# Local attention scores of a tile in one step over four PSUM banks instead of two steps over two banks each

## The chip, the cores and the metric

The kernel runs on one core of a Trainium2 chip, as one launch. The metric is the device time of the launch in microseconds (us), lower is better. Engines are named as in the profile: PE is TensorE (PEld its weight loads), DVE is VectorE, ACT is ScalarE, POOL is GpSimd, SP is SyncE, which issues nearly all DMAs.

## The reference

One layer of a streaming encoder on 2048 prompt tokens and 8 x 16 tokens of running streams (17 tiles of 128 tokens), model width 1024, all in float32. What the change touches is the local attention of the prompt: 8 query heads share 2 key/value heads of width 64, a chunk of 64 tokens sees itself and the two chunks before it, and each head has a learned sink in the softmax's denominator.

```python
def band_attend(q, k, v, mask, sinks):
    s = jnp.einsum('bnlkgd,bnskd->bnkgls', q, k) * (A_HEAD_DIM ** -0.5)
    s = jnp.where(mask, s, -jnp.inf)
    mx = jnp.maximum(jnp.max(s, axis=-1, keepdims=True), sink)
    p = jnp.exp(s - mx)
    p = p / (jnp.sum(p, axis=-1, keepdims=True) + jnp.exp(sink - mx))
    return jnp.einsum('bnkgls,bnskd->bnlkgd', p, v)
...
qm, km, vm, om, ip, fp, qa, ka, va = split_in(x @ w_in)
hm = og * head_norm(mlstm_chunkwise(...))          # matrix memory, 4 heads x 128
ha = swa_prompt(rope(qa), rope(ka), va, attn_sinks)
mix = jnp.concatenate([hm, ha], axis=-1) @ w_out
h = layer_norm(DEEPNORM_ALPHA * x + mix, ln1_g, ln1_b)
f = conv_ffn(h, ...)                               # up, causal convolution, silu gate, down
y = layer_norm(DEEPNORM_ALPHA * h + f, ln2_g, ln2_b)
```

## The kernel before

**Stages.** Four follow each other on TensorE. The input projection (`i_dense`, lines L770 and L798) goes over four blocks of tokens. The output projection (`o_block`, L232 to L234) goes over five blocks, [16, 0, 1], [2..5], [6..9], [10..13] and [14, 15], counted here from 0 to 4. Then come the feed-forward's up projections (`f_ups`, L1949) and down projections (`f_downs`, L2153). Products in float32 are made of three products of a high and a low part (`split`: ScalarE casts to the high part at L227, VectorE subtracts for the low part at L228). The matmuls of these stages are called dense here; their banks are named dps, fup and fht.

**Chains.** The sequence part runs between the dense matmuls of the first two stages, as three generators: `t_sample` (the running streams), `m_chain` (the matrix memory of the prompt, tile by tile) and `a_chain` (the local attention of the prompt, tile by tile). `Chains.weave` keeps a clock of its own: each dense piece adds its cost in nanoseconds, and a chain makes its next step when its due time has come. A step yields (its cost on TensorE, the delay until its next step, the number of banks that the next step needs).

**Banks.** Chains share five PSUM banks (`NBANKS`, pool `tps`). Each request (`bank`) enters in a list when the planner holds that bank to be free again: now plus `HOLDS[name]`, or 3500 ns for a name that isn't there. A step that needs n banks waits until the n oldest entries have passed. TensorE's order is written down as the program is made; the order on the other engines is set by a scheduler from the program's order and its own estimates of time. [...]

**One tile of attention** (`swa`). `swa_first` turns queries and keys by transposes (pq, pk) and splits them. `scores(j0)` makes two of the four query heads of each key head: 12 matmuls into two banks (psc, L1389, operands of 64 rows), then mask and row maximum on VectorE (L1393, one operation per head, into sc), then the sink. `exps` takes the exponentials on ScalarE (L1404), `divided` the quotients (L1410). The probabilities are turned by TensorE (ppt, L1432), copied by ScalarE (pth, L1433) and multiplied with the values (ppo, L1438); a copy (mixa, L1445) and a DMA to zmix end the tile. The steps stand like this:

```python
z = [scores(0)]
yield 900, 3200, 2
exps(*z[0])
z.append(scores(2))
yield 900, 3600
exps(*z[1])
divided(*z[0])
...
yield 0, 3000
divided(*z[1])
```

Of the matrix memory's tile the text names pscore and pkt (L1215, L1226), pnum and pcu (L1300 on), pgr (rows of gates, L1073), pht (turned result, L1267; ScalarE copies it to mixm at L1270) and pcol (L1092; VectorE copies it to col at L1095).

**From the chains to the next stage.** Output block b + 1 reads zmix in four pieces (`x_pair`, DMA xraw), which are cast (oh, L965) and reduced to low parts (ol, L966, VectorE or POOL; VectorE alone for block 4) in the last round of block b. `x_pair` first lets the chains run on until the tiles that it reads are written. Its results are added to the input (ymix, L1724), normed in steps (`norm`: L1657, L1647 to L1650, L1661, L1663) and stored to zh. Once no chain is left, block 3's loop frees the chains' memory and banks and starts `prepare`: ScalarE issues six loads of normed tiles (hst, L1801), 18 steps later TensorE transposes them (fht, L1810) and ScalarE copies them (hraw, L1811), one transpose group per step, and then the first feed-forward block's tokens are summed and split (`f_tokens`: hraw at L1825 to L1829, hh and hl of 1536 columns), one such piece every four steps. The loop over block 4 goes on with `prepare`, and after it an assertion says that `prepare` is finished.

Of the kernel before, what the change touches and what calls it, by code (L numbers as in the profile page):

```python
# [14 lines left out]
P = 128  # L15
# [16 lines left out]
RING = 3  # L32

NBANKS = 5
HOLDS = {"pm": 6500, "pgr": 4000, "pnum": 5000, "ppo": 6500}

WB = 4

# [166 lines left out]
class Prog:  # L205
# [30 lines left out]
    def run(self):  # L236
        PS = bass.MemoryType.PSUM
        nb = len(OBLOCKS)
        with ExitStack() as es:
            def enter(*a, **k):  # L240
                cm = self.pool(*a, **k)
                return cm.__enter__(), cm
            close = lambda cm: cm.__exit__(None, None, None)
            self.cp = es.enter_context(self.pool("const"))
            self.dp = es.enter_context(self.pool("dram", space=bass.MemoryType.DRAM))
            es.enter_context(self.tc.manual_schedule(engines={mybir.EngineType.PE}))
            self.setup()
            self.wp = es.enter_context(self.pool("wsb"))
            self.dps = es.enter_context(self.pool("dps", 3, PS))
            self.tp, tcm = enter("tsb", side="right")  # L250
            self.tps, tpcm = enter("tps", 5, PS)
            self.xp, xcm = enter("xsb")
            self.skew(self.xp, 256)
            self.mp, mcm = enter("isb")
            chains = Chains(self)
            self.xs, self.gates, self.i_done = {}, {}, 0
            self.i_begin()
            self.warm_up()
            chains.weave(self.i_dense())
            close(mcm)  # L260
            wx, wxcm = enter("wx1sb")
            self.skew(wx, 448)
            self.unit_more(wx)
            self.mp, mcm = enter("osb")
            self.o_setup()
            for b in range(nb - 2):
                chains.weave(self.late_done(self.o_block(b)))

            def prepare():
                first = self.f_hT(0)  # L270
                next(first)
                for _ in range(18):
                    yield
                for _ in first:
                    yield
                for s in (1, "t1", "t3", 7, "t2", 6):
                    self.f_tokens(0, s)
                    for _ in range(4):
                        yield

            made, n = None, 0
            for cost in self.late_done(self.o_block(nb - 2)):
                chains.weave([cost])
                if made is None:
                    if not chains.live:
                        close(tpcm)
                        close(tcm)
                        self.fp, fcm = enter("fsb", side="right")
                        self.fup, fpcm = enter("fup", 3, PS)
                        self.f_setup()  # L290
                        made = prepare()
                else:
                    next(made, None)
            assert made is not None
            for i, _ in enumerate(self.o_block(nb - 1)):
                next(made, None)

                if i >= 22 and n < (2, 4, 5)[min((i - 22) // 4, 2)]:
                    self.f_next()
                    n += 1  # L300
            assert next(made, self) is self and not self.norms
            close(mcm)
            close(wxcm)
            close(xcm)

            self.wx, wxcm = enter("wx2sb")
            self.skew(self.wx, 704)
            self.f2, f2cm = enter("f2sb")
            self.f3, f3cm = enter("f3sb")
            self.f_ups(n)  # L310
            self.skew(self.f2, 448)
            close(f3cm)
            close(f2cm)
            self.f2, f2cm = enter("dsb")
            self.f_downs()
            for cm in (f2cm, wxcm, fpcm, fcm):
                close(cm)
# [678 lines left out]
    def bank(self, shape, name):  # L996
        self.chains.ask(HOLDS.get(name, 3500))
        return self.tps.tile(shape, F32, name=name, tag="tb")
# [360 lines left out]
    def swa(self, t):  # L1359
        nc = self.nc  # L1360
        V = nc.vector
        if self.a_first is None:
            self.swa_first(t)
            yield 550, 4000, 2
        qh, ql = self.a_first
        self.a_first = None
        r = t % RING
        if t == 0:
            slots, nk = [0], 1
            mask = self.mswa[:, :P]  # L1370
            sel = slice(0, 1)
        else:
            slots, nk = sorted([(t - 1) % RING, r]), 2
# [5 lines left out]
        def scores(j0):  # L1379

            sink = [x.rearrange("p (k j) -> p k j", k=2)[:, :, j0:j0 + 2] for x in (self.sink, self.nsink)]
            sc = self.work("sc", [P, 4, 2 * P], bufs=2)
            mx, es, sm = [self.work(n, [P, 4], bufs=2) for n in ("amx", "aes", "asm")]
            ps = [self.bank([P, 2, 2, P], "psc") for _ in range(2)]
            for j in range(2):
                for i, (q, k) in enumerate(((qh, self.kh), (qh, self.kl), (ql, self.kh))):
                    for kvh in range(2):
                        rs = slice(64 * kvh, 64 * kvh + 64)
                        nc.tensor.matmul(ps[kvh][:, j, :nk], q[rs, j0 + j], k[rs, sel], start=i == 0, stop=i == 2)  # L1389
            for kvh in range(2):  # L1390
                for j in range(2):
                    c = 2 * kvh + j
                    V.tensor_tensor_reduce(out=sc[:, c, :N], in0=ps[kvh][:, j, :nk].rearrange("p a b -> p (a b)"), in1=mask, scale=1.0, scalar=-3e38,  # L1393
                                           op0=ALU.add, op1=ALU.max, accum_out=mx[:, c:c + 1])

            w = lambda x: x.rearrange("p (k j) -> p k j", k=2)
            V.scalar_tensor_tensor(w(mx), w(mx), -0.125, sink[1], op0=ALU.mult, op1=ALU.min)
            V.tensor_add(w(es), sink[0], w(mx))
            return sc, mx, es, sm

        def exps(sc, mx, es, sm):
            nc.scalar.activation(es, es, AF.Exp)
            for j in range(4):
                nc.scalar.activation(sc[:, j, :N], sc[:, j, :N], AF.Exp, bias=mx[:, j:j + 1], scale=0.125, accum_out=sm[:, j:j + 1])  # L1404

        def divided(sc, mx, es, sm):
            V.tensor_add(sm, sm, es)
            V.reciprocal(sm, sm)
            for j in range(4):
                nc.scalar.activation(sc[:, j, :N], sc[:, j, :N], AF.Copy, scale=sm[:, j:j + 1])  # L1410

        z = [scores(0)]
        yield 900, 3200, 2
        exps(*z[0])
        z.append(scores(2))
        yield 900, 3600
        exps(*z[1])
        divided(*z[0])
        if t + 1 < NPT and self.i_done > self.place(t + 1)[0]:
# [7 lines left out]
        for kt in range(nk + 1):  # L1427
            new = self.work("pth", [P, 2, 512], bufs=2) if kt < nk else None
            for kvh in range(2) if kt < nk else ():
                pp = self.bank([P, 512], "ppt")  # L1430
                for j in range(4):
                    nc.tensor.transpose(pp[:, j * P:(j + 1) * P], scs[j // 2][:, 2 * kvh + j % 2, kt * P:(kt + 1) * P], self.ident)  # L1432
                nc.scalar.copy(new[:, kvh], pp)  # L1433
            if kt:
                po = po or self.bank([P, 512], "ppo")
                for kvh in range(2):
                    w = self.kv[slots[kt - 1]][:, P + 64 * kvh:P + 64 * kvh + 64]
                    nc.tensor.matmul(po[64 * kvh:64 * kvh + 64], w, pts[:, kvh], start=kt == 1, stop=kt == nk)  # L1438
            pts = new
            if kt == 0 and self.a_load is not None:  # L1440

                self.swa_first(t + 1)
                self.chains.t += 550
            yield (860 if kt < nk else 0) + (1400 if kt else 0), 0 if kt == nk else 1500 if kt else 3000, 2 * (kt + 1 < nk) + (kt == 0)
        nc.scalar.copy(mix.rearrange("p a b -> p (a b)"), po)  # L1445
        self.mix_out(t, 4, mix)

# [797 lines left out]
```

## Time and profile before

| | |
|---|---|
| time, three runs | 2298.55 us median (2301.94, 2297.17, 2298.55) |
| profiled execution | 2297.75 us, span of its instructions 2295.9 us |
| busy share of the span | PE 99%, PEld 91%, DVE 78%, ACT 57%, POOL 10% |
| matmuls in the trace | 14332 |
| granted TensorE clock, mean | 0.999 of full speed |
| DMA | 629.22 MB, mean 274 GB/s |
| score matmuls (psc) | 384, first at 296.3 us, last at 827.0 us |
| mask and maximum (sc<-psc) | 128 on VectorE, median 418 ns |

The span is the time from the first to the last instruction of one execution; what remains to the execution's own time, 1.85 us, lies around it. A row of the timeline has its start in us from the span's start, its duration, the engine, the line, the operation, output<-inputs, the shapes, how many instructions it merges, and in brackets the engine's idle time before it with what ended it. Matmuls overlap in a pipeline, so the distance between two starts says more than a duration. In rows of waits the numbers are the total, how often, and the longest.

### The profile page before, as it was taken

What the parts mean: (1) busy time and instruction counts of PE and PEld (TensorE: products, weight loads), DVE (VectorE), ACT (ScalarE), POOL (GpSimd) and SP (SyncE); (2) the same over time, 40 slices, a digit from 0 to 9 for tenths busy, and PEclk for the clock granted to TensorE, in tenths of its full rate; (3) what the DMA queues carried; (4) which work ended last, traced back from release to release, by engine and by line L of the source; (5) the groups of instructions that cost most, each with busy time, mean ns of one, the idle gap of its engine ahead of it and who ended that gap; (6) DMA issues with size and microseconds to landing.
All of it is one profiled execution on the core that took longest, in us unless ns stands there. A gap on an engine that the chain in (4) does not pass through costs nothing.

```text
span 2295.9 us, 39756 instructions
## 1 busy us (share of the span) xinstructions
PE 2263.9 (99%) x14332; PEld 2086.8 (91%) x14332; DVE 1798.4 (78%) x3157; ACT 1307.0 (57%) x2465; POOL 226.0 (10%) x289
## 2 busy tenths in 40 slices
PE   8999999999999999999999999999999999999998
PEld 8999988989878778999999999999999988888887
DVE  8777687787688879987888666778766787796897
ACT  5463466776866655555556555555555644654753
POOL 0001001001122222100002000002000000000100
PEclk9999999999999999999999999999999999999999
DMA  7898899999977756787767899887988786757653
GB/s 279 304 324 308 286 307 325 324 327 312 324 277 245 246 196 249 286 320 289 278 270 259 281 316 319 307 305 275 322 292 263 236 289 219 244 194 231 241 186 110
DMA packets 299796, 629.22 MB, mean 274 GB/s; under 512 B 47372, under 2 KB 140624, under 8 KB 299600
## 3 DMA queue, kind: packets, MB, share of 16 engines
q1 hardware_dynamic: 298736, 623.55, 78.1%
q10 hardware_dynamic: 864, 3.15, 0.4%
q8 instruction: 113, 1.85, 0.3%
q14 instruction: 83, 0.68, 0.1%
HBM read 456.01 MB, written 170.59 MB: 273 GB/s over the span
## 4 chain that ended last, share of the span: by engine, by line
PE 84%; DVE 6%; DMA 4%; ACT 2%; issue 2%; POOL 1%; SPq 0%; DVEq 0%; ACTq 0%; POOLq 0%
PE dps L1949 19%; PE fup L1949 19%; PE dps L770 12%; PE dps L2153 7%; PE fht L2153 6%; PE fup L2153 6%; PE dps L232 3%; PE dps L234 2%; PE dps L233 2%; DMA txy<-wdn 1%; PE ppo L1438 1%; PE psx L782 1%; PE dps L798 1%; DVE w L228 1%; PE psc L1389 1%
## 5 line engine op out<-in xcount | busy, mean ns | idle before, releaser
L1949 PE MATMUL dps<-hh,uw 128*128 128x384 f32 (+1 forms) x1848 | 477.5, 327 | 5.3 <-DVE u L1982 2.6
L1949 PE MATMUL fup<-hh,uw 128*128 128x384 f32 (+1 forms) x1848 | 476.5, 326 | 0.0
L1997 DVE SCALAR_TENSOR_TENSOR cc<-u,cw,cc 128x768 f32<-128x768 f32 (+1 forms) x264 | 257.7, 977 | 124.6 <-ACT cc L1995 121.2
L1949 PEld LDWEIGHTS dps<-hh,uw 128*128 128x128 f32 x1848 | 329.2, 188 | 7.6 <-DVE u L1982 3.2
L1949 PEld LDWEIGHTS fup<-hh,uw 128*128 128x128 f32 x1848 | 329.2, 188 | 0.1
L1949 PE MATMUL fup<-hl,uw 128*128 128x384 f32 (+1 forms) x924 | 301.3, 326 | 1.0 <-DVE hl L228 1.0
L1949 PE MATMUL dps<-hl,uw 128*128 128x384 f32 (+1 forms) x924 | 301.0, 326 | 0.0
L770 PE MATMUL dps<-w,oh 128*128 128x256 f32 x1344 | 252.9, 283 | 1.9 <-DMA w<-zws 1.3
L770 PEld LDWEIGHTS dps<-w,oh 128*128 128x128 f32 x1344 | 210.6, 189 | 14.3 <-issue 8.9
L228 DVE TENSOR_TENSOR w<-wraw,w 128x1024 fp32r<-128x1024 f32 (+1 forms) x155 | 182.0, 1179 | 51.5 <-ACT w L227 50.1
L227 ACT CAST uw<-wraw 128x1024 fp32r<-128x1024 f32 x126 | 123.2, 981 | 173.3 <-PE dps L2153 104.1
L227 ACT CAST w<-wraw 128x1024 fp32r<-128x1024 f32 (+1 forms) x155 | 155.7, 1009 | 88.4 <-PE dps L770 39.2
L228 DVE TENSOR_TENSOR uw<-wraw,uw 128x1024 fp32r<-128x1024 f32 x126 | 142.4, 1130 | 64.0 <-ACT uw L227 63.8
L770 PE MATMUL dps<-w,ol 128*128 128x256 f32 x672 | 187.2, 279 | 0.0
L1995 ACT ACTIVATE cc<-u,cw 128x768 f32<-128x768 f32 (+1 forms) x132 | 131.9, 999 | 95.7 <-DVE u L1991 92.8
L1949 PEld LDWEIGHTS fup<-hl,uw 128*128 128x128 f32 x924 | 173.5, 188 | 1.8 <-DVE hl L228 1.8
L1949 PEld LDWEIGHTS dps<-hl,uw 128*128 128x128 f32 x924 | 173.5, 188 | 0.0
L770 PE MATMUL dps<-oh,w 128*128 128x256 f32 x896 | 169.4, 284 | 4.1 <-ACT zev L839 1.5
L2153 PE MATMUL fup<-uw,fu 128*128 128x512 f32 x726 | 169.0, 389 | 0.0
L2153 PEld LDWEIGHTS fup<-uw,fu 128*128 128x128 f32 x726 | 136.2, 188 | 28.2
L2153 PE MATMUL dps<-uw,fu 128*128 128x512 f32 x660 | 160.9, 389 | 0.1
L770 PEld LDWEIGHTS dps<-oh,w 128*128 128x128 f32 x896 | 140.6, 188 | 11.6 <-issue 4.9
(348 smaller groups left out, 4557.8 us busy)
## 6 DMA issues: line engine op xcount, KB each, us to landing
uw<-zw SPq DMA_DIRECT2D x176, 512.0 KB
zw<-uw SPq DMA_DIRECT2D x88, 512.0 KB
w<-zws SPq DMA_DIRECT2D x72, 512.0 KB
wv<-wup SPq DMA_DIRECT2D x66, 512.0 KB
wraw<-wi SPq DMA_DIRECT2D x62, 512.0 KB
wraw<-zt SPq DMA_DIRECT2D x60, 512.0 KB
wraw<-wdn SPq DMA_DIRECT2D x45, 512.0 KB
wraw<-wo SPq DMA_DIRECT2D x40, 512.0 KB
```

The source lines that it names most:

```text
L227: nc.scalar.copy(hi, src)
L228: nc.vector.tensor_sub(lo, src, hi.bitcast(F32))
L232: mm(out, ah, bh, start=start, stop=False)
L233: mm(out, ah, bl, start=False, stop=False)
L234: self.mark = mm(out, al, bh, start=False, stop=stop)
L770: self.mark = mm(o, l, r, start=s in (1, 7) and c == k == i == 0, stop=k == 3 and i == 2, skip_group_check=True)
L782: mm(o, x[:, k], w[:, k], start=s == 1 and k == i == 0, stop=s in (2, 4) and k == 3 and i == 2, skip_group_check=True)
L798: mm(o, x, w, start=k == i == 0, stop=k == KD - 1 and i == 2, skip_group_check=True)
L1949: mm(ps, l[:, k], r[:, k], start=s in (1, 7) and k == 0 and i == 0, stop=k == 3 and i == 2, skip_group_check=True)
L1995: S.activation(c[:, v], u[:, v, 2:2 + n], AF.Identity, bias=w[3], scale=w[2])
L1997: V.scalar_tensor_tensor(c[:, v], u[:, v, i:i + n], w[i], c[:, v], op0=ALU.mult, op1=ALU.add)
L2153: mm(ps, l[:, k, c], r[:, k], start=s in (1, 4, 7) and u == 0 and k == 0 and i == 0, stop=u == nu - 1 and k == n - 1 and i == 2, skip_grou ...
```

## The change

Both calls of `scores` are made in one step, which asks for four free banks at once; the second half's banks get a name and a hold time of their own (psc2, 5500 ns). The delays of the following steps are set anew. Since the next tile's scores may follow the last step of a tile directly, this step asks for four banks too. The assertion on `prepare` gives way to a loop that finishes it. No instruction is added or taken away; what changes is the order on each engine. Later line numbers go up by two at the most.

```diff
-HOLDS = {"pm": 6500, "pgr": 4000, "pnum": 5000, "ppo": 6500}
+HOLDS = {"pm": 6500, "psc2": 5500, "pgr": 4000, "pnum": 5000, "ppo": 6500}
...
-            assert next(made, self) is self and not self.norms
+            for _ in made:
+                pass
+            assert not self.norms
...
             self.swa_first(t)
-            yield 550, 4000, 2
+            yield 550, 4000, 4
...
-            ps = [self.bank([P, 2, 2, P], "psc") for _ in range(2)]
+            ps = [self.bank([P, 2, 2, P], f"psc{j0}") for _ in range(2)]
...
-        z = [scores(0)]
-        yield 900, 3200, 2
+        z = [scores(0), scores(2)]
+        yield 1600, 3200
         exps(*z[0])
-        z.append(scores(2))
-        yield 900, 3600
+        yield 0, 1800
         exps(*z[1])
         divided(*z[0])
...
-            yield (860 if kt < nk else 0) + (1400 if kt else 0), 0 if kt == nk else 1500 if kt else 3000, 2 * (kt + 1 < nk) + (kt == 0)
+            yield (860 if kt < nk else 0) + (1400 if kt else 0), 0 if kt == nk else 1500 if kt else 3000, 4 if kt == nk else 2 * (kt + 1 < nk) + (kt == 0)
```

Three places in the order at which this shows are quoted where the prediction uses them: TensorE around a tile's scores, and ScalarE and VectorE around the beginning of output block 4.

## The prediction

> **What bounds the kernel now.** I read the profile's page first, then windows of the stage that the change touches, then the waits of TensorE there.
>
> ```profile
> span 2295.9 us, 39756 instructions
> PE 2263.9 (99%) x14332; PEld 2086.8 (91%) x14332; DVE 1798.4 (78%) x3157; ACT 1307.0 (57%) x2465; POOL 226.0 (10%) x289
> PE 84%; DVE 6%; DMA 4%; ACT 2%; issue 2%; POOL 1%; SPq 0%; DVEq 0%; ACTq 0%; POOLq 0%
> ```
>
> TensorE is busy for 99% of the span and carries 84% of the chain of work. The change adds and removes no instruction: each engine's count in the built program is the same. So it can act in three ways only: TensorE's time for the same matmuls in another order, the gaps in which it waits, and what the later end of the chains does to the next stage. The stage runs from 296 us (first score) to 832 us; the hand-over to the feed-forward part follows.
>
> ```profile
> 296.00:870.00 574.00, 563.66 (x4045) 484.19 (x4044) 456.56 (x1332) 383.23 (x1004) 91.92 (x75) 1.00 0.85 289
> 864.00:904.00 40.00, 39.89 (x199) 32.34 (x198) 36.98 (x43) 21.62 (x29) 4.82 (x3) 1.00 0.67 237
> 904.00:926.00 22.00, 21.02 (x125) 20.20 (x124) 22.00 (x29) 15.85 (x24) 14.09 (x3) 1.00 0.71 263
> ```
>
> The columns are the stretch, its length, then busy time of PE, PEld, DVE, ACT and POOL. In the chain stage TensorE is idle for 574.00 - 563.66 = 10.3 us. In the 40 us ahead of the feed-forward it has no gap to speak of. At the start of the feed-forward it loses 22.00 - 21.02 = 1.0 us, while VectorE is busy for all 22.00 of 22.00.
>
> ```profile
> PE pnum L1300 <- DVE sd L1220: 1.7, 1, 1.7
> PE ppt L1432 <- ACT pth L1433: 1.6, 2, 0.9
> PE pgr L1073 <- DVE C L1311: 1.2, 1, 1.2
> PE ppt L1432 <- DVE ay L1159: 1.1, 1, 1.1
> ```
>
> These are the longest of TensorE's waits between 290 and 870 us (total, times, longest). No score matmul (psc) is among them, and none recurs per tile. "Two banks instead of four" is not what TensorE waits for today.
>
> **Term 1: one visit instead of two.** In TensorE's order, at tile 15, the first 12 score matmuls stand between dense matmuls (dps) before:
>
> ```order
> L232 MATMUL dps<-w,oh 128x512
> L233 MATMUL dps<-w,oh 128x512
> L234 MATMUL dps<-w,ol 128x512
> L1389 MATMUL psc<-kringh,qh 128x256 x2
> L1389 MATMUL psc<-kringl,qh 128x256 x2
> L1389 MATMUL psc<-kringh,ql 128x256 x2
> L1389 MATMUL psc<-kringh,qh 128x256 x2
> L1389 MATMUL psc<-kringl,qh 128x256 x2
> L1389 MATMUL psc<-kringh,ql 128x256 x2
> L232 MATMUL dps<-w,oh 128x512
> L233 MATMUL dps<-w,oh 128x512
> L234 MATMUL dps<-w,ol 128x512
> ```
>
> and after, the first half's last rows run straight into the second half's (line numbers are shifted by one or two):
>
> ```order
> L1391 MATMUL psc_11431<-kringl,qh 128x256
> L1391 MATMUL psc_11430<-kringh,ql 128x256
> L1391 MATMUL psc_11431<-kringh,ql 128x256
> L1391 MATMUL psc_11454<-kringh,qh 128x256
> L1391 MATMUL psc_11455<-kringh,qh 128x256
> L1391 MATMUL psc_11454<-kringl,qh 128x256
> L1391 MATMUL psc_11455<-kringl,qh 128x256
> ```
>
> The dense matmuls that stood between are still there, elsewhere. What a visit costs is read from TensorE's timeline (start, duration; both visits of tile 15):
>
> ```profile
> 821.40 0.40 PE L234 MATMUL dps<-w,ol 128*128 128x512 f32 x1
> 821.73 0.39 PE L1389 MATMUL psc<-kringh,qh 64*128 64x256 f32 x2
> 821.95 0.28 PE L1389 MATMUL psc<-kringl,qh 64*128 64x256 f32 x2
> 822.42 0.28 PE L1389 MATMUL psc<-kringh,ql 64*128 64x256 f32 x2
> 822.63 0.50 PE L232 MATMUL dps<-w,oh 128*128 128x512 f32 x1
> 823.20 0.40 PE L234 MATMUL dps<-w,ol 128*128 128x512 f32 x1
> 826.00 0.40 PE L234 MATMUL dps<-w,ol 128*128 128x512 f32 x1
> 826.33 0.39 PE L1389 MATMUL psc<-kringh,qh 64*128 64x256 f32 x2
> 827.80 0.40 PE L234 MATMUL dps<-w,ol 128*128 128x512 f32 x1
> ```
>
> From 823.20 to 826.00 lie 12 dense steps: 0.233 us each. From 821.40 to 823.20 is 1.80 us with three dense steps in it (0.70), so the visit costs 1.10; the second (826.00 to 827.80) the same. Its six pairs follow each other at (822.42 - 821.95)/4 = 0.117 us: 0.70. So 0.40 us of each visit is entering and leaving. Ten of the sixteen tiles run beside narrower dense matmuls; there:
>
> ```profile
> 613.85 0.28 PE L770 MATMUL dps<-w,oh 128*128 128x256 f32 x1
> 615.30 0.39 PE L770 MATMUL dps<-w,oh 128*128 128x256 f32 x2
> 618.37 0.28 PE L770 MATMUL dps<-w,oh 128*128 128x256 f32 x1
> ```
>
> 27 dense steps from 615.30 to 618.37 make 0.114 each; 613.85 to 615.30 is 1.45, less three steps 1.11, less 0.70: 0.41. The merged visit pays this once: 16 tiles x 0.40 = **-6.4 us**, on the path. [...]
>
> **Term 2: waits inside the stage.** With the new bank counts the planner puts 198 instead of 186 dense matmuls into a tile's period (counted in the order). Softmax gets more room, so ppt's two rows above (2.7 us) could go; eight mask-and-maximum operations now come in one burst on VectorE, which can delay others. I take 0, with -3 and +4 as ends: the gain is ppt's two rows, and the loss is their sum with pgr's row, rounded up.
>
> **Term 3: the chains end later, and the next stage's preparation with them.** By the order the last chain instruction on TensorE (ppo's second group) comes 51 dense matmuls later, 51 x 0.233 = 11.9 us. The feed-forward starts at the same dense matmul as before. The token preparation, made when the chains are done, therefore starts at the 57th instead of the 36th of the 72 steps of output block 3, and its transposes fall into block 4. Two queues matter. First ScalarE, at the end of the chains; before:
>
> ```order
> L1445 COPY mixa<-ppo 128x512
> L1801 DMA hst<-zh_181 128x1024
> L1801 DMA hst<-zh_182 128x1024
> L1801 DMA hst<-zh_183 128x1024
> L1801 DMA hst<-zh_184 128x1024
> L1801 DMA hst<-zh_185 128x1024
> L1801 DMA hst<-zh_186 128x1024
> L1811 COPY hraw<-fht 128x4x128 x2
> L965 CAST oh<-xraw 128x2x256
> ```
>
> and after:
>
> ```order
> L1446 COPY mixa<-ppo 128x512
> L227 CAST w<-wraw 128x1024
> L1802 DMA hst<-zh_181 128x1024
> L1802 DMA hst<-zh_182 128x1024
> L1802 DMA hst<-zh_183 128x1024
> L1802 DMA hst<-zh_184 128x1024
> L1802 DMA hst<-zh_185 128x1024
> L1802 DMA hst<-zh_186 128x1024
> L967 CAST oh<-xraw 128x2x256
> L227 CAST w<-wraw 128x1024
> ```
>
> The six loads are still ahead of the casts of block 4's tokens (oh), but block 4 now begins 48 dense matmuls, 11.2 us, after the chains' end. The trace says how long the loads hold ScalarE (one row of TensorE, one of SyncE's queue, three of ScalarE):
>
> ```profile
> 852.31 1.08 PE L1438 MATMUL ppo<-pth,kva 128*64 128x512 f32 x4
> 855.32 0.39 SPq L1261 DMA_DIRECT2D zmix<-mixa  x1
> 853.49 0.61 ACT L1445 COPY mixa<-ppo 128x512 f32<-128x512 f32 x1
> 859.91 6.22 ACTq L1801 DMA_DIRECT2D hst<-zh  x6
> 866.17 0.59 ACT L1811 COPY hraw<-fht 128x512 f32<-128x512 f32 x1 [12.07 <-PE fht L1810]
> ```
>
> From ppo's end (about 853.3) to 866.1 is 12.8 us. So the first token cast ends near 12.8 + 0.6 = 13.4 us after the chains' end, where TensorE would ask for it at 11.2: 2.2 us late. Second, VectorE, which makes the low parts (ol), around the same place; before:
>
> ```order
> L966 TENSOR_TENSOR ol<-xraw,oh 128x2x256
> L1825 TENSOR_TENSOR hraw<-hraw 128x4x384
> L228 TENSOR_TENSOR w<-wraw,w 128x1024
> L966 TENSOR_TENSOR ol<-xraw,oh 128x2x256
> L1724 SCALAR_TENSOR_TENSOR ymix<-ymix,dps 128x512 x2
> L228 TENSOR_TENSOR w<-wraw,w 128x1024
> ```
>
> and after:
>
> ```order
> L1725 SCALAR_TENSOR_TENSOR ymix<-ymix,dps 128x512 x2
> L1648 BN_STATS lst<-ymix 128x6 x2
> L1649 BN_AGGR lmv<-lst 128x2 x2
> L1650 TENSOR_SCALAR lsc<-lmv 128x1
> L1662 SCALAR_TENSOR_TENSOR ymix<-ymix,lmv,o_ln_g 128x1024
> L968 TENSOR_TENSOR ol<-xraw,oh 128x2x256
> L1664 SCALAR_TENSOR_TENSOR ymix<-ymix,lsc,o_ln_b 128x1024
> L228 TENSOR_TENSOR w<-wraw,w 128x1024
> L968 TENSOR_TENSOR ol<-xraw,oh 128x2x256
> ```
>
> Before, all four ol stood ahead of the pair of adds that read block 3's last two banks; now none does, and these adds wait for block 3's last matmul, the one right ahead of block 4's first. Prices, from VectorE's timeline:
>
> ```profile
> 869.57 0.68 DVE L966 TENSOR_TENSOR ol<-xraw,oh 128x512 fp32r<-128x512 f32 x1
> 881.03 0.69 DVE L966 TENSOR_TENSOR ol<-xraw,oh 128x512 fp32r<-128x512 f32 x1
> 881.63 1.28 DVE L1724 SCALAR_TENSOR_TENSOR ymix<-ymix,dps 128x512 f32<-128x512 f32 x2
> 882.83 1.22 DVE L228 TENSOR_TENSOR w<-wraw,w 128x1024 fp32r<-128x1024 f32 x1
> 883.96 1.75 DVE L1827 TENSOR_TENSOR hraw<-hraw 128x1536 f32<-128x1536 f32 x1
> 885.63 1.28 DVE L1647 BATCH_NORM_STATS2 lst<-ymix 128x6 f32<-128x512 f32 x2
> 886.83 0.19 DVE L1648 BATCH_NORM_AGGREGATE lmv<-lst 128x2 f32<-128x12 f32 x1
> 887.75 0.15 DVE L1649 TENSOR_SCALAR lsc<-lmv 128x1 f32<-128x1 f32 x1
> 887.81 1.28 DVE L1661 SCALAR_TENSOR_TENSOR ymix<-ymix,lmv,o_ln_g 128x1024 f32<-128x1024 f32 x1
> 890.67 1.28 DVE L1663 SCALAR_TENSOR_TENSOR ymix<-ymix,lsc,o_ln_b 128x1024 f32<-128x1024 f32 x1
> ```
>
> The first ol ends 1.28 + 1.28 + 2 x 0.19 + 0.15 + 1.28 + 0.68 = 5.05 us after block 3's end. TensorE needs it at block 4's third matmul, 2 x 0.23 = 0.47 us in: it stands still for 4.6 us. The second ol follows 1.28 + 1.22 + 0.68 = 3.2 us later; TensorE has six matmuls (1.4 us) until it asks: 1.8 us more. The third comes 1.9 us after that, beside six matmuls and by then two of the transposes: covered. So 6.4 us at block 4's start. VectorE itself then stands before the feed-forward with four more long rows than before (two hraw, two hl, about 4 x 1.75 = 7.0 us), against which it has won the 6.4 us of the stall and the time of the transposes now in block 4. I therefore count the 1.0 us that TensorE loses at the feed-forward's start today as gone or kept, and book 0.5. Against overlapping row ends (some 0.08 us each) I round the term to **+5 us**. Its ends are +2 (ScalarE's lateness alone) and +9.
>
> **Sum.** -6.4 + 0 + 5 = -1.4 us. The profiled execution took 2297.75 us (span 2295.9), which gives 2296.4; the median of the three runs shown is 0.8 us higher, so I say **2296.5 us**. The runs shown spread by 4.8 us, so about 0.2% (4.6 us) is what a measurement of this kernel can tell from no change.
>
> **Rivals.** (a) Clearly faster: block 4's start costs only its +2 and ppt's 2.7 us go: -6.4 + 2 - 2.7 = -7.1, about 2290.7. For it: the terms are the lower ends of rows. Against it: VectorE works in order, so 5.05 us holds unless its queue has slack that the order doesn't show.
>
> (b) Slower by SyncE's queue: block 4's third and fourth token loads now stand behind a store of the norm's result (zh) and a load into its buffer, which waits for a landed store. Bounds and the rival's bank wait:
>
> ```profile
> SPq L1697 <- DMA zh<-ymix: 17.5, 5, 8.2
> 330.50 0.25 PE L1092 MATMUL pcol<-ident,ay 36*128 36x36 f32 x1
> 333.31 0.18 DVE L1095 COPY col<-pcol 128x36 f32<-128x36 f32 x1
> ```
>
> The first row is that wait between 800 and 920 us, up to 8.2 us. It decides if the fourth load lands later than the 6.4 us of stall and the 4.2 us of the first six k-steps leave; at the full 8.2 us: -1.4 + 8.2 = +6.8, 2304.6 us.
>
> (c) The scores wait for banks. In the built program the second half's banks are those that pht and pcol had, so its matmuls wait for a ScalarE and a VectorE copy. The two rows show the slowest kind of copy: 3.0 us from pcol to its end. After, the second half comes some 3.5 us behind pcol (ppo 1.0, 12 dense steps 1.4, half a visit 0.9, seams), so nothing waits. If VectorE's burst made it 1 us late in 15 tiles, it would be 2296.4 + 15 = 2311, since a tile then takes four of the five banks at once. [...]
>
> (d) The 0.40 us is no seam and comes back elsewhere: 0 + 5, 2302.8 us.
>
> **Chances.** Forecast 0.52; (a) 0.25; (b) 0.13; (c) 0.04; (d) 0.06. So faster by over 0.2%: 0.25, within: 0.52, slower: 0.23. The range runs from 2289.5 (just below (a)) to 2304.5 ((b) nearly in full, (d) inside); the likeliest case alone lies between 2294 and 2303.
>
> **What would show it.** Right: one score run of 24 per tile of about 1.8 us with its seams, TensorE idle for 4 to 7 us at block 4's start with ol as the releaser, no more than 1 us at the feed-forward's start. Wrong: psc among TensorE's waits on every tile; ol in time, since another order of events keeps VectorE ahead; or a stall at block 3's start, whose tokens the chains now deliver just in time too.

## The result, and the profile after

The changed kernel takes 2307.04 us (median of five runs, 2306.02 to 2311.19), the kernel before on the same chip 2298.55 us. The ratio is 1.0039, 95% interval 1.0028 to 1.0050: slower by 8.5 us, outside the predicted range. A second measurement on another chip gave 1.0035 (1.0022 to 1.0048). The profiled execution took 2310.16 us; it is compared with the profiled 2297.75 us of before, 12.4 us apart. That is more than the 8.5 us between the medians, since the profile after lies at the slow end of its runs and the one before at the fast end of its own. Runs of one kernel spread by 4 to 13 us, so terms of 2 or 3 us are read from profiles and only larger ones from the runs. Two of the twelve runs of two_visits_pnum4000, an experiment below, were slow (4456 and 4540 us), and its ratio is that of the other ten.

The page after, and TensorE by stretches (columns as before; the third row is block 4, the fourth the start of the feed-forward):

```profile
span 2308.4 us, 39737 instructions
PE 2264.7 (98%) x14332; PEld 2088.4 (90%) x14332; DVE 1802.6 (78%) x3157; ACT 1304.4 (57%) x2465; POOL 226.3 (10%) x289
```

```profile
296.00:870.00 574.00, 556.03 (x4013) 480.69 (x4013) 455.06 (x1323) 377.67 (x997) 91.96 (x74) 0.99 0.83 284
870.00:882.00 12.00, 11.66 (x49) 8.47 (x49) 6.56 (x11) 1.64 (x2) 1.44 (x1) 1.00 0.87 273
882.00:918.00 36.00, 31.69 (x158) 25.40 (x159) 32.67 (x40) 21.18 (x31) 2.89 (x2) 0.95 0.70 261
918.00:940.00 22.00, 21.61 (x125) 20.79 (x124) 22.00 (x27) 15.43 (x22) 15.75 (x3) 1.00 0.49 179
```

TensorE's busy time is as before (2264.7 against 2263.9 us). Its idle time in the chain stage went from 10.3 to 574.00 - 556.03 = 18.0 us, block 4 has 4.6 us where there was next to none (4.3 in the third row, and 0.3 of its first wait in the second), and the feed-forward's start has 0.4 instead of 1.0. The length of the feed-forward has not changed: it begins 12.4 us later (916.11 against 903.74 us), and the last matmul starts 12.4 us later too (2300.40 against 2287.99 us).

The merged visit of tile 15, from the timeline:

```profile
840.76 0.40 PE L234 MATMUL dps<-w,ol 128*128 128x512 f32 x1
841.09 0.39 PE L1391 MATMUL psc<-kringh,qh 64*128 64x256 f32 x2
842.71 0.50 PE L232 MATMUL dps<-w,oh 128*128 128x512 f32 x1
843.28 0.40 PE L234 MATMUL dps<-w,ol 128*128 128x512 f32 x1
```

From 840.76 to 843.28 is 2.52 us; less three dense steps (0.70) the visit of 24 matmuls costs 1.82 us, where two visits of 12 cost 2 x 1.10. Over all tiles the means are 1.10 (32 visits, before) and 1.81 us (16 visits, after): 6.2 us were saved. They were spent elsewhere. TensorE's longest waits between 290 and 950 us:

```profile
PE dps L772 <- ACT dps L849: 3.5, 1, 3.5
PE dps L234 <- POOL v L1185: 3.3, 2, 1.8
PE dps L772 <- ACT dps L870: 3.0, 2, 2.0
...
PE dps L232 <- ACT oh L967: 1.9, 1, 1.9
PE dps L234 <- POOL ol L968: 1.8, 1, 1.8
PE dps L234 <- DVE ol L968: 1.7, 2, 1.5
```

Before, no row exceeded 1.7 us, and the longest were on chain matmuls. Now they are on dense ones. No score matmul (psc) waits. What was added belongs to three places.

**Output blocks 1 to 3.** Around block 2's start (744.96 us) in the timeline of TensorE and GpSimd:

```profile
753.96 0.50 PE L234 MATMUL dps<-w,ol 128*128 128x512 f32 x1 [1.50 <-POOL v L1185]
```

```profile
751.46 2.45 POOL L968 TENSOR_TENSOR ol<-xraw,oh 128x1024 fp32r<-128x1024 f32 x1 [8.22 <-ACT oh L967]
753.85 0.11 POOL L1185 MEMSET v<- 128x4 f32 x1
```

The row of waits names a memset; the instruction meant is the low part (ol) right ahead of it on GpSimd, and that one waited for its cast on ScalarE. Why the cast was late is seen 70 us earlier, at block 1 (start 674.99 us), in ScalarE's timeline:

```profile
669.77 0.51 ACT L1406 ACTIVATE sc<-sc,amx 128x256 f32<-128x256 f32 x1 [2.58 <-DVE amx L1399]
674.86 1.70 ACT L1412 ACTIVATE sc<-sc,asm 128x256 f32<-128x256 f32 x4
677.40 1.04 ACT L967 CAST oh<-xraw 128x1024 fp32r<-128x1024 f32 x1
678.35 1.70 ACT L1412 ACTIVATE sc<-sc,asm 128x256 f32<-128x256 f32 x4
680.89 1.05 ACT L967 CAST oh<-xraw 128x1024 fp32r<-128x1024 f32 x1
```

From 669.8 us on ScalarE works without a gap through the exponentials and quotients of the tile in flight; the last two casts of the block's tokens stand between them. Before, the block's last two casts began 7.25 and 4.25 us ahead of its first matmul; now 2.4 and 5.9 us behind it. The chains' data is not late there: the result of tile 5, the last that block 1 needs, is copied (mixa) at 520.3 us, 155 us ahead of the block, and tile 9's 83 us ahead of block 2. At block 3 the data is close as well: tile 13's is copied 12 us ahead of the block, where it was 33. TensorE loses 1.8, 1.5 and 2.6 us at the three starts.

**The input projection.** Tile 0's softmax in ScalarE's timeline:

```profile
304.82 0.40 ACT L1406 ACTIVATE sc<-sc,amx 128x128 f32<-128x128 f32 x1 [7.59 <-DVE amx L1399]
306.99 0.40 ACT L1406 ACTIVATE sc<-sc,amx 128x128 f32<-128x128 f32 x1 [0.42 <-DVE amx L1399]
307.38 0.58 ACT L849 COPY dps<-dps 128x512 f32<-128x512 f32 x1
```

L849 copies a dense bank to another, and TensorE goes on in it. Before, this copy stood ahead of the first exponential (at 300.39 us); now five of them stand ahead of it, and ScalarE idles for 7.59 us for a row maximum with the copy behind it. TensorE waits 3.5 us. Later in this stage it waits 3.0 us more for the same kind of copy (L870; 0.6 before) and 2.2 us for weight loads (w<-zws; no such row before), while its waits on chain matmuls shrank.

**Block 4.** TensorE, and ScalarE with its queue:

```profile
883.53 0.50 PE L232 MATMUL dps<-w,oh 128*128 128x512 f32 x1 [1.87 <-ACT oh L967]
885.73 0.80 PE L234 MATMUL dps<-w,ol 128*128 128x512 f32 x1 [1.46 <-DVE ol L968]
893.51 0.66 PE L1811 MATMUL fht<-ident,hst 128*128 128x128 f32 x4 [1.32 <-ACT hraw L1812]
```

```profile
873.91 8.90 ACTq L1802 DMA_DIRECT2D hst<-zh  x6
882.86 0.62 ACT L967 CAST oh<-xraw 128x512 fp32r<-128x512 f32 x1 [8.50 <-DMA wraw<-wo]
892.35 0.62 ACT L967 CAST oh<-xraw 128x512 fp32r<-128x512 f32 x1 [3.15 <-DMA xraw<-zmix]
892.88 0.58 ACT L1812 COPY hraw<-fht 128x512 f32<-128x512 f32 x1
```

The six loads hold ScalarE for 8.9 us, and the first token cast begins 11.9 us after ppo's last group ended on TensorE (870.97 us). The third wait (1.32 us, for a bank of the transposes) has another origin: the copy that empties this bank (L1812) stands behind the fourth token cast, for whose load ScalarE idled 3.15 us. SyncE had issued this load only at 882.53 us, right behind the load into the norm's buffer, which had waited 5.1 us for a landed store.

**The clock.** TensorE in two pieces of 3.41 us, around the wait at tile 0 and behind it (the third column from the right is the granted clock):

```profile
305.13:308.54 3.41, 0.53 (x4) 0.53 (x5) 3.33 (x21) 2.99 (x13) 0.00 (x0) 1.00 1.05 305
308.54:311.95 3.41, 3.41 (x18) 3.41 (x18) 2.74 (x5) 3.41 (x14) 0.00 (x0) 0.50 0.89 353
```

After the wait the granted clock is 0.50 for 3.41 us. A dense step takes 0.213 us in that stretch (308.84 to 309.48 us for three) and 0.113 us behind it (312.01 to 312.35); from the clock I estimate the cost at 0.50 x 3.41 = 1.7 us on top. This happens three times after the change (from 308.5, 499.7 and 885.4 us, 4.9 us of busy time in all) and once before (572.9 us, 1.6 us), and a busy column does not show it.

From the first score to the first feed-forward matmul, profile against profile: 607.4 us before, 619.8 after, +12.4. Of that -6.2 are the visits, +12.2 idle time (3.1 in the input projection, 4.5 in the output blocks, 4.6 at block 4) and +3.3 clock; the remaining 3.1 us I could not place.

### The profile page after: what moved, and what is told of

The parts are those of the page before. It is cut to its first block, busy times and chain, and to the rows that moved or that the text cites. A ratio compares the mean times of both kernels' runs of the same rounds, so it can differ in the third digit from the quotient of the medians.

```text
span 2308.4 us, 39737 instructions
## 1 busy us (share of the span) xinstructions
PE 2264.7 (98%) x14332; PEld 2088.4 (90%) x14332; DVE 1802.6 (78%) x3157; ACT 1304.4 (57%) x2465; POOL 226.3 (10%) x289
## 3 DMA queue, kind: packets, MB, share of 16 engines
q10 hardware_dynamic: 864, 3.15, 0.4%
## 4 chain that ended last, share of the span: by engine, by line
PE 71%; DVE 5%; DMA 3%; issue 3%; ACT 2%; POOL 1%; SPq 0%; DVEq 0%; POOLq 0%; ACTq 0%
PE fup L1950 18%; PE dps L1950 18%; PE dps L2154 6%; PE fup L2154 6%; PE fht L2154 6%; PE dps L772 5%; PE dps L232 2%; PE dps L234 2%; PE dps L233 2%; PE ppo L1439 1%; PE psc L1391 1%; PE ppt L1433 1%; PE dps L800 1%; DVE uw L228 1%; DMA xraw<-zmix 1%
```

## The experiments

Theory A (place): the merged visit saves what was forecast, and the loss comes from where the planner's new bank demands put the chains' steps against the dense matmuls. Theory B (burst): merging itself costs, since masks and exponentials now come eight at a time. The table has each kernel's ratio to the kernel before measured beside it, the length from first score to first feed-forward matmul in its profile, and TensorE's idle time there (input projection / output blocks 0 to 3 / from 4 us ahead of block 4 to the feed-forward), from windows cut at these instants. The profiled execution of the kernel before took 2297.75 us, where its medians beside the later kernels were 2302.1 to 2303.4. So small differences of length against its row mean little, and the ratios decide.

| kernel | visits | last attention step in block 3 (of 72) | ratio, 95% interval | length, us | idle, us |
|---|---|---|---|---|---|
| before | 2 | 36 | 1 | 607.4 | 8.6 / 1.8 / 0.0 |
| after | 1 | 57 | 1.0039 (1.0028 to 1.0050) | 619.8 | 11.7 / 6.3 / 4.6 |
| after_again | 1 | 57 | 1.0035 (1.0022 to 1.0048) | 620.6 | 11.7 / 6.3 / 4.3 |
| two_visits_late | 2 | 57 | 1.0064 (1.0050 to 1.0078) | 626.0 | 11.5 / 5.9 / 4.6 |
| two_visits_pnum4000 | 2 | 34 | 0.9981 (0.9971 to 0.9991) | 609.3 | 9.2 / 3.6 / 0.0 |
| two_visits_early | 2 | 7 | 1.0003 (0.9994 to 1.0012) | 610.8 | 10.1 / 1.7 / 0.0 |
| one_visit_pnum4000 | 1 | 32 | 0.9986 (0.9976 to 0.9995) | 611.8 | 14.7 / 3.6 / 0.0 |
| one_visit_early | 1 | 21 | 0.9961 (0.9946 to 0.9975) | 605.6 | 10.1 / 2.9 / 0.0 |
| one_visit_earlier | 1 | 14 | 1.0122 (1.0109 to 1.0136) | 641.7 | 20.3 / 10.7 / 0.4 |

**Late chains without the merging (two_visits_late).** The kernel before, with one demand more, and the rest of `prepare` finished by the loop of the change:

```diff
-            yield (860 if kt < nk else 0) + (1400 if kt else 0), 0 if kt == nk else 1500 if kt else 3000, 2 * (kt + 1 < nk) + (kt == 0)
+            yield (860 if kt < nk else 0) + (1400 if kt else 0), 0 if kt == nk else 1500 if kt else 3000, 3 if kt == nk else 2 * (kt + 1 < nk) + (kt == 0)
```

> The kernel before, two score visits of 12 per tile, but the last step of a tile asks for three free banks instead of none; the last attention step then stands at step 57 of output block 3's 72 steps, as in the changed kernel, and what is left of the preparation is finished after block 4, as there. Theory A (place): nothing is saved at the scores, and the late chains cost some 4 us net at the starts of blocks 1 to 3, 5 us at block 4 and 0 to 4 us in the input projection: 2307 to 2312 us. Theory B (burst): only block 4's start costs, about 5 us: 2302 to 2305 us.

Measured: 2316.71 us against 2303.11, +13.6 (by the ratio +14.7), at and above the top of theory A's range, far from B's. Of its four longest rows of waits three are of the changed kernel's kind, with no score merged; the first, on the matrix memory's chain, is its own:

```profile
PE pnum L1302 <- DVE sd L1222: 4.7, 2, 2.6
PE dps L772 <- ACT dps L870: 4.2, 1, 4.2
PE dps L232 <- ACT oh L967: 3.2, 1, 3.2
PE dps L234 <- DVE ol L968: 2.7, 2, 1.4
```

So the later place costs more without the merging than the whole change does, and at the late place the merging is a gain: 1.0064 to 1.0039, some 6 us, and 626.0 to 619.8 us between the profiles.

**The planner's number set back (one_visit_pnum4000), and its control (two_visits_pnum4000).** The changed kernel, and the kernel before, each with

```diff
-HOLDS = {..., "pnum": 5000, "ppo": 6500}
+HOLDS = {..., "pnum": 4000, "ppo": 6500}
```

> The changed kernel with one number of the planner's bank list set back: pnum is held 4000 instead of 5000 ns. The scores stay in one visit over four banks, but the last attention step now stands at step 32 of output block 3's 72 steps (36 before the change, 57 with it). Theory A (place: the loss comes from where the chains' steps fall against the dense matmuls, so that casts of tokens stand behind softmax work on ScalarE at the starts of output blocks 1 to 3 and the preparation falls into block 4): the 7.5 us of stalls at the starts of blocks 1 to 3 and the 5.0 us at block 4 go back to what they were before (about 2), the 6.3 us of the merged visits stay saved, some 3 to 5 us of stalls in the input projection stay: 2295 to 2297 us, about 0.1% faster than before. Theory B (burst: eight mask-and-maximum operations and eight exponentials in one go hold VectorE and ScalarE wherever they fall): no gain over the changed kernel, 2304 to 2309 us.

> The kernel before with pnum held 4000 instead of 5000 ns, two score visits per tile; the last attention step stands at step 34 of 72 (36 before). It shows what the planner's number does without the merging. Theories A and B both: within 2 us of the kernel before, 2296.5 to 2300.5 us.

Measured: 0.9986, some 3 us faster than before, as theory A has it, and for the control 0.9981, some 4 us below the kernel before, which neither theory expected. Block 4's wait and most of those at the block starts are gone (3.6 / 0.0), as A says. But beside its control the merging gains nothing here: the input projection idles for 14.7 us against 9.2. Its two longest waits are again for bank copies on ScalarE, 3.3 us at L849 and 3.0 us at L870. The wait for L849 stands in the profiles of all eight kernels that merge tile 0 (2.7 to 5.9 us) and in none of the six that don't. So theory B holds a part: at tile 0 the merging itself puts softmax in front of a copy that dense matmuls wait for. The wait for L870 is not tied to the merging: two_visits_late has 4.2 us of it, one_visit_early 0.6.

**One visit, early chains (one_visit_early).** As one_visit_pnum4000, and

```diff
-... 4 if kt == nk else 2 * (kt + 1 < nk) + (kt == 0)
+... 2 if kt == nk else 2 * (kt + 1 < nk) + (kt == 0)
```

> As the kernel with pnum at 4000 ns, and the last step of a tile asks for two banks instead of four; the last attention step stands at step 21 of output block 3's 72. Theory A (place): the block starts depend on the phase of the softmax against them, which here is another one; block 4 keeps its old cover: 2292 to 2297 us. Theory B (burst): 2304 to 2309 us.

Measured: 2292.09 us against 2303.11; ratio 0.9961, about 9 us faster than the kernel before, where theory A had 2 to 7. TensorE in block 4 (to 902 us):

```profile
870.00:902.00 32.00, 32.00 (x139) 25.64 (x138) 31.93 (x41) 14.43 (x17) 4.28 (x3) 1.00 0.59 197
```

Not one gap in block 4. This is the version to keep: the merging of the change, with two numbers of the planner other than it chose.

**Early chains with two visits (two_visits_early).** The kernel before with pnum at 4000 and

```diff
-        yield 900, 3600
+        yield 900, 2600
```

> Two score visits per tile, pnum held 4000 instead of 5000 ns, and 2600 instead of 3600 ns after the second visit: the last attention step stands at step 7 of output block 3's 72 (36 before, 57 in the changed kernel). Theory A (place): with the chains that early no block waits for tokens, as with one visit and early chains, but no seam is saved: 6 us above the one with one visit, that is 2 to 4 us below the kernel before. Rival (early chains alone do not matter and all of the gain of the one with early chains came from the seams): within 1.5 us of the kernel before. Second rival (softmax asked for too early: TensorE waits at ppt): above the kernel before.

Measured: 1.0003. The first rival is right: the chains of before were early enough. By these pairs the merging is worth 1.0003 - 0.9961 = 0.42% at an early place (about 9.7 us, more than its 6.2) and 0.25 to 0.29% (about 6 us) at the late one, but nothing with pnum alone at 4000 (0.9981 against 0.9986). The early pair stands at two different steps (7 and 21); against the fastest kernel with two visits, two_visits_pnum4000, the version to keep gains 0.20%, some 4.6 us. With one visit the late place costs 0.74 to 0.78% (17 us), with two 0.61% (14 us).

**Banks asked for too few (one_visit_earlier).** As one_visit_early, and

```diff
-        yield 0, 4200, 2 + 2 * (self.a_load is not None)
+        yield 0, 3600, 2
```

> One visit, pnum 4000 ns, two banks at a tile's end, and ahead of the turned probabilities 3600 instead of 4200 ns and two banks instead of four: the last attention step stands at step 14 of 72 (21 in the kernel with early chains). Theory A: as that kernel or up to 2 us faster, since its stalls at block starts are nearly gone already: 9 to 12 us below the kernel before. Rival (banks: the planner's demand of four protects TensorE): waits at ppt, pq or pk by several us, 3 to 8 us below the kernel before.

Measured: 1.0122, 28 us slower than before, outside both figures.

```profile
PE dps L772 <- ACT zev L841: 9.6, 8, 2.7
PE dps L772 <- ACT dps L870: 4.4, 3, 2.1
PE dps L772 <- ACT dps L849: 3.7, 1, 3.7
```

Earlier is not better in itself. Most of the waits are not for banks of the chains, as the rival had it, but again for ScalarE's copies of dense banks (17.7 us in three rows).

**Block 4's queues (after_blk4, after_blk4_gp).** The changed kernel; after_blk4 has the first two edits, after_blk4_gp all three:

```diff
-                (nc.sync if b else nc.scalar).dma_start(hs[ti], self.zh[tiles[ti]])
+                nc.sync.dma_start(hs[ti], self.zh[tiles[ti]])
...
-        (nc.gpsimd if b < nb - 1 and p % 2 else nc.vector).tensor_sub(l, raw, h.bitcast(F32))
+        (nc.gpsimd if p % 2 else nc.vector).tensor_sub(l, raw, h.bitcast(F32))
...
-        nc.sync.dma_start(raw, self.zmix[b][2 * p:2 * p + 2].rearrange("k p m -> p k m"))
+        (nc.gpsimd if b == nb - 1 else nc.sync).dma_start(raw, self.zmix[b][2 * p:2 * p + 2].rearrange("k p m -> p k m"))
```

> The changed kernel with two edits at output block 4 only: SyncE instead of ScalarE issues the six loads of normed tiles (hst), and GpSimd instead of VectorE makes the low parts (ol) of the second and fourth token piece. Theory A (the 5.0 us stall at block 4's start comes from ScalarE held by its six loads and from VectorE's order): the stall shrinks to 1 to 2 us, so 3 to 4 us below the changed kernel, that is 5 to 6 us above the kernel before. Rival (the tokens themselves land late, whoever casts them): the stall stays, 8 to 9 us above the kernel before.

> The changed kernel with three edits at output block 4: SyncE issues the six loads of normed tiles (hst), GpSimd's queue issues the four token loads (xraw), and GpSimd makes every second low part (ol). Theory A (block 4's tokens are late because of the queues that they stand in; in the kernel that freed ScalarE alone, the third and fourth load stood on SyncE behind the load into the norm's buffer and TensorE waited 10.7 us): with a queue of their own all four pieces are cast before TensorE asks, the stall at block 4 shrinks to under 2 us, 4 to 5 us below the changed kernel. Rival (the pieces land late, since the last tile is written late): a stall of 4 us or more stays and the time is that of the changed kernel within 2 us.

Measured: after_blk4 1.0066 (1.0053 to 1.0079), against both theories. ScalarE was free and cast the first two pieces early, but the other two came later than ever. TensorE's wait, ScalarE and SyncE's queue:

```profile
PE dps L232 <- ACT oh L967: 11.3, 2, 10.7
```

```profile
895.42 0.62 ACT L967 CAST oh<-xraw 128x512 fp32r<-128x512 f32 x1 [9.30 <-DMA xraw<-zmix]
890.33 0.33 SPq L1698 DMA_DIRECT2D ymix<-x  x1
890.71 0.95 SPq L963 DMA_DIRECT2D xraw<-zmix  x2
```

Loads three and four stood on SyncE behind the load into the norm's buffer. That is the prediction's rival (b), met in a kernel that took ScalarE's hold away. With a queue of their own (after_blk4_gp) no matmul of block 4 waits for tokens (0.4 us is left, for a bank of the transposes), as theory A says, yet the ratio is 1.0026 (1.0015 to 1.0037), only 2 us below the changed kernel: the preparation is still late, and a wait came back at the start of the feed-forward, 3.3 us for ScalarE's copy of a bank (L1963), with a granted clock of 0.84 over the first 22 us.

**Token casts of blocks 1 to 3 on VectorE (after_oh_dve).**

```diff
-        nc.scalar.copy(h, raw)
+        (nc.vector.tensor_copy if 0 < b < nb - 1 else nc.scalar.copy)(h, raw)
```

> The changed kernel with the casts of tokens (oh) of output blocks 1 to 3 made by VectorE instead of ScalarE. Theory A (the casts stand behind the softmax on ScalarE, which the changed kernel's trace shows busy without a gap from 11 us before block 2's first matmul on): the 7.5 us of stalls at the starts of blocks 1 to 3 shrink to 1 to 3 us, so 4 to 6 us below the changed kernel, 3 to 5 us above the kernel before. Rival (the token loads land late, because the chains write their tiles late): no change, 8 to 9 us above. A third way: VectorE, which stands in order too, gets late with the masks instead; then the stalls move to ppt and the time stays above the changed kernel's.

Measured: in its profile (the fastest of its nine runs, 2304.20 against a median of 2310.98 us) the waits at the starts of blocks 1 and 2 are gone and block 3's remains (1.2 and 1.6 us for oh and ol), but small waits elsewhere make up for them: the output blocks idle for 5.9 us against 6.3. The ratio, 1.0037 (1.0025 to 1.0049), is that of the changed kernel. None of the three theories fits: the stalls at blocks 1 and 2 went as A says but the time did not, and they did not move to ppt (0.2 us) as the third way has it.

**Tile 0 back in two visits (after_t0_two, early_t0_two).**

```diff
-        z = [scores(0), scores(2)]
-        yield 1600, 3200
-        exps(*z[0])
-        yield 0, 1800
+        if t:
+            ...
+        else:
+            z = [scores(0)]
+            yield 900, 3200, 2
+            exps(*z[0])
+            z.append(scores(2))
+            yield 900, 3600
```

> The changed kernel with tile 0 alone back to two score visits; the fifteen other tiles keep one visit, and the planner's place of the last attention step is the same (57 of 72). On ScalarE the copy of a dense bank (dps to dps) then stands ahead of tile 0's first exponential, as before the change, instead of behind five of them. Theory A: the stall of 5.2 us at 304 us goes back to about 2, one seam of 0.4 us comes back: 2.5 to 3.5 us below the changed kernel, 5.5 to 6.5 us above the kernel before. Rival (the stall there is the clock or chance): no change, 8 to 9 us above.

> The kernel with one visit and early chains (pnum 4000 ns, two banks at a tile's end), and tile 0 alone in two visits. In that kernel the profile shows 8.4 us of stall at tile 0. Theory A: about 6 us of it go, one seam of 0.4 us comes back: 5 to 6 us below the kernel with early chains, that is 13 to 15 us below the kernel before. Rival (no order on ScalarE behind it): as the kernel with early chains, 8 to 10 us below the kernel before.

Measured: 1.0039 (1.0026 to 1.0053) and 0.9966 (0.9953 to 0.9978), each as its kernel without the edit. The wait for L849 is gone in both profiles, and in both the stage is 1.8 us shorter (619.8 to 618.0, 605.6 to 603.8), where 2.5 to 6 us were expected. What shows next in the second is a wait of the matrix memory's pnum for VectorE, 2.0 us. The runs cannot tell 1.8 us from nothing.

**The changed kernel once more (after_again).**

> The changed kernel once more, beside the three kernels of this call. All theories: 8 to 10 us above the kernel before (ratio 1.003 to 1.005), TensorE idle for 16 to 19 us between 296 and 870 us and for 3 to 5 us at output block 4.

Measured: 1.0035, and the idle times of the table: as expected, but for a wait of 5.4 us instead of 3.5 at tile 0.

## Why the prediction was wrong, point by point

- **What bounds the kernel** (TensorE; not the banks of the scores): right. psc waits in neither kernel's list.
- **Term 1, one visit instead of two**, -6.4 us: right, -6.2 measured visit by visit; whole kernels agree at the late place (about 6 us), show more at the early one and nothing with pnum at 4000. So rival (d), by which all of it comes back elsewhere, is not the rule; part of the 3.1 us without a place could still be of its kind. No run shows what the 0.40 us of entering and leaving is made of; 2 x 1.10 - 1.81 = 0.39 us a tile is what the merged visits were measured to save.
- **Term 2, waits inside the chain stage**, 0 with -3 and +4: this is the step that failed. Idle time there grew by 7.6 us, and clock losses by 1.8. The forecast read which chain matmuls wait today and asked what the merging does to them. It did not ask what the later place does to the dense matmuls: which of ScalarE's and GpSimd's instructions for them fall behind a tile's softmax. The price in idle time is 4.5 us in the output blocks (6.3, of which 5.9 at the three starts, against 1.8 before) and 3.1 us in the input projection. The forecast named a stall at block 3's start as what would make it wrong and gave it no price; blocks 1 and 2 it did not consider, since their tiles are finished long before. What is late there is not the data but the cast.
- **Term 3, the chains end later**, +5 with +2 and +9: right in place, and in size partly by luck. Block 4 idles 4.6 us more, the clock adds 1.5, and the feed-forward's start gains 0.6: +5.5. The parts were weighed wrongly. ScalarE is late by 1.9 us (forecast 2.2), but VectorE's order costs 1.5, where the forecast had 6.4 for the two together: TensorE was already late and the adds ran beside that. Two things that were not forecast fill the gap, the wait of 1.3 us for a bank of the transposes and the clock.
- **Rivals**: (a) needed term 3 to be small. (b) is in the result with a small price, the 1.3 us for the bank whose copy stood behind the late fourth load, and decides once ScalarE is out of the way (after_blk4). (c) did not occur.
- **The clock** was in no term: 3.3 us of the 12.4.
- **Range**: its upper end held one mechanism at a time. The result is terms 1 and 3 near the forecast and a term 2 of more than twice its upper end, 7.6 + 1.8 = 9.4 us. Up to the feed-forward's first matmul that makes -6.2 + 9.4 + 4.6 + 1.5 = +9.3 us, to which the profiles add the 3.1 that have no place; the 0.6 us gained behind it is lost again further on.

What stays open: 3.1 us between the two profiles; and why the merging gains nothing with pnum at 4000 beside its control, of which the profile shows only that the difference lies in the input projection, with two waits of 3.3 and 3.0 us for bank copies. Also, the edits that took away one kind of wait each (at block 4, at blocks 1 and 2, at tile 0) brought the changed kernel's time back by 2 us at most; only moving the chains did more. So the runs show the place as a whole as the cause of the loss, while the price of each wait is read from the trace.

## What to carry to other kernels

When a change moves the place of side work against a saturated engine, price the moved place by what each in-order queue now holds ahead of the saturated engine's own next operands, at every hand-over, and not only by whether the data is finished in time (here ScalarE idled for 7.59 us with the copy behind it that TensorE waited 3.5 us for). Then separate the two: keep the new form and set the place back by the planner's numbers, and keep the old form at the new place; here the form gained 6 us at the late place, 10 at an early one and nothing at a third, and the late place cost 14 or more. Freeing one queue at a crowded hand-over may only show the next one; the wait moved from ScalarE to SyncE to the feed-forward's start.

## What the runs showed of the hardware

In the traces of before and after every change of the granted clock lies on a border of stretches of 3.41 us, and whether half clock follows goes, in the rows here, with how long TensorE was busy in one stretch and not with how long a single wait was. Two pairs of stretches of the kernel after, each with the stretch that follows:

```profile
496.28:499.69 3.41, 1.38 (x12) 1.17 (x11) 3.38 (x8) 2.27 (x5) 0.00 (x0) 1.00 0.76 281
499.69:503.10 3.41, 3.41 (x18) 3.41 (x17) 2.41 (x3) 2.59 (x5) 0.00 (x0) 0.50 1.07 346
680.60:684.01 3.41, 2.12 (x9) 1.11 (x7) 3.41 (x12) 1.51 (x3) 2.00 (x1) 1.00 0.77 241
684.01:687.42 3.41, 2.91 (x14) 2.28 (x15) 3.21 (x14) 0.17 (x1) 1.26 (x3) 1.00 0.99 315
```

The first holds the whole of a wait of 2.03 us, the third most of one of 1.78 us. In one_visit_pnum4000 a wait of 3.31 us (303.3 to 306.6 us) falls across two stretches, and the clock stays full, in the stretch behind them too:

```profile
301.59:305.00 3.41, 1.72 (x16) 1.52 (x14) 2.82 (x13) 1.75 (x9) 1.28 (x1) 1.00 1.04 331
305.00:308.41 3.41, 1.79 (x15) 1.79 (x16) 2.90 (x14) 2.81 (x10) 0.00 (x0) 1.00 0.89 324
308.41:311.82 3.41, 3.41 (x32) 3.41 (x32) 2.48 (x6) 3.41 (x12) 0.00 (x0) 1.00 0.77 278
```

In after_again a wait of 1.80 us, with part of one of 0.54 us in the same stretch, is enough:

```profile
820.53:823.94 3.41, 1.29 (x4) 0.78 (x5) 2.99 (x14) 0.51 (x3) 2.46 (x1) 1.00 0.84 298
823.94:827.35 3.41, 3.41 (x9) 2.64 (x8) 2.20 (x6) 0.00 (x0) 1.35 (x1) 0.50 0.07 26
```

So in these rows a stretch at full clock in which TensorE was busy for 1.38 us or less was followed by half clock, and one with 1.72 us or more was not. Over all stretches of before and after from 10 us on, the busiest that half clock followed had 1.49 us (569.43 us, before), and the least busy that it did not follow 1.66 us (1574.89 us, after). A wait through the whole stretch was not needed: 2.03 of 3.41 us of idle time were followed by half clock. By the estimate above a half-clock stretch of busy TensorE costs 1.7 us, in rows that count as busy.
